# Gate and up products of a decoder's feed-forward blocks: seven block products in place of eight

## The chip, the cores and the metric

One core of a Trainium2 chip runs the whole kernel. The metric is the device time of one execution in microseconds (us). Matrix products run on TensorE (PE for the matmuls, PEld for their weight loads), elementwise work on VectorE (DVE) and ScalarE (ACT), a few DMA starts on GpSimd (POOL); SyncE (SP) starts the other DMAs.

## The reference, cut to what matters

Two layers, each with a feed-forward block, a mixer of four branches, and a second feed-forward block; x is 512 tokens by 1024 features, in float32, and D_FF is 2816.

```python
def _swiglu(x, w_gate, w_up, w_down):
    return (jax.nn.silu(x @ w_gate) * (x @ w_up)) @ w_down
...
for l in range(DEPTH):
    x = x + 0.5 * _swiglu(_rmsnorm(x, ffn1_norm[l]), ffn1_w_gate[l], ffn1_w_up[l], ffn1_w_down[l])
    ...
    x = x + 0.5 * _swiglu(_rmsnorm(x, ffn2_norm[l]), ffn2_w_gate[l], ffn2_w_up[l], ffn2_w_down[l])
```

The change touches `x @ w_gate` and `x @ w_up` in the four feed-forward blocks.

## The kernel before, in words

Activations lie transposed: x is eight tiles of 128 features by 512 tokens. Every float32 operand is split into a high part rounded to float32r and a low rest (`split`, L228: a cast on ACT, a subtraction on DVE), and a product is three matmuls (`mm3`, L223): high by high, high by low, low by high. Each matmul loads 128x128 weights and streams 512 tokens past them.

A feed-forward block (`ffn`, L327) has 22 tiles of 128 hidden features. For one tile, `proj` (L303) makes the gate product and the up product, 8 x 3 matmuls each, into two banks of the pool "mm" (4 banks; another 4 are "bg"). `hidden` (L330) multiplies both by the row factor of the norm (`st.rb`), applies silu, multiplies, and splits the result into two `L` tiles. After 12 tiles, and after the other 10 (`HALVES`, L30), `down` (L315) multiplies the hidden tiles by `w_down` into four banks at a time and adds them to x. The last `down` of a block also prepares the input of the next stage (`norm_split`, L269), and a small generator computes its row factor. In the mixer, `renorm` (L292) rewrites the split input during the third projection.

Weights come as chunks of 128x1024 (512 KB). `nextw` (L215) hands out the next one and keeps two more in work: `load_one` (L181) starts the DMA into one of two `ws` buffers and splits it into one of three `wh` and three `wl`. A buffer comes free when its last reader is through: `wh` and `wl` when the matmuls of that chunk are, `ws` when the subtraction is. At the start of the first block `setup` (L372) builds the attention bias with a DMA to DRAM (`toep`, L389) and back.

The order in which each engine takes its instructions is not that of the program: the library's planner runs through the program with costs of its own, gives each engine the earliest written instruction that is then ready, and that order is fixed in the queues. Waits are on semaphores; an instruction that waits holds all behind it in its queue.

Of the kernel before, what the change touches and what calls it, by code (L numbers as in the profile page):

```python
# [13 lines left out]
F32 = mybir.dt.float32  # L15
# [14 lines left out]
HALVES = ((0, 12), (12, 22))  # L30
# [36 lines left out]
def _trunk(tc, xin, wst, wa, wv, wf, par, relb, cst, out):  # L67
# [8 lines left out]
    def T(shape, dt, tag, bufs=1):  # L76
        uid[0] += 1
        n = int(np.prod(shape[1:])) * (2 if dt == BF16 else 4)
        return (odd if n % 2048 else sb).tile(shape, dt, tag=tag, bufs=bufs, name=f"{tag}_{uid[0]}")
# [18 lines left out]
    def LT(i, dt=F32R):  # L98
        return T([P, S], dt, f"L{i}")
# [60 lines left out]
    sched = []  # L160
    ci = 0
    per_ffn = 2 * NF + 2 * (NF // 2)
    for l in range(2):
        stream = ["w"] * per_ffn
        for z in ZORDER:
            stream += [z] * 4 if z in GROUPS else ["w"]
        stream += ["w"] * (4 * (2 + 8) + 8 + per_ffn)
        kc = {z: 4 * l for z in GROUPS}
        for z in stream:
            if z == "w":  # L170
                sched.append((1024, wst[ci]))
                ci += 1
            else:
                sched.append((2 * GROUPS[z], wg[z][kc[z]]))
                kc[z] += 1
    assert ci == nchunk
    loaded = deque()
    pos = [0]
    AHEAD = 2

    def load_one():  # L181
        n, src = sched[pos[0]]
        pos[0] += 1
        st = T([P, 1024], F32, "ws", 2)[:, 0:n]
        wh = T([P, 1024], F32R, "wh", 3)[:, 0:n]
        wl = T([P, 1024], F32R, "wl", 3)[:, 0:n]
        nc.sync.dma_start(st, src)
        split(wh, wl, st)
        loaded.append((wh, wl))

    def load_first():

        ts_ = []
        for i in range(2):
            pos[0] += 1
            ts_.append((T([P, 1024], F32, "ws", 2), T([P, 1024], F32R, "wh", 3), T([P, 1024], F32R, "wl", 3)))
# [15 lines left out]
        loaded.extend(t[1:] for t in ts_)  # L212
        spawn(norm_end(st))

    def nextw():  # L215
        while len(loaded) <= AHEAD and pos[0] < len(sched):
            load_one()
        return loaded.popleft()
# [49 lines left out]

    def norm_split(st, k):  # L269
        g = pc(st.l, st.off + k)  # L270
        hi = T([P, S], F32R, f"xh{k}")
        lo = T([P, S], F32R, f"xl{k}")
# [19 lines left out]
    def renorm(st):  # L292

        st.x = []
        for k in range(KD):
            y = TP()
            hi = T([P, S], F32R, f"xh{k}")
            lo = T([P, S], F32R, f"xl{k}")
# [28 lines left out]
    def ffn(st, nxt, fin=None, first=False):  # L327
        for hi_, (t0, t1) in enumerate(HALVES):
            hs = []
            def hidden(t, pg, pu, rb):  # L330
                sg, us = TP(), TP()
                V.tensor_mul(sg, pg, rb)  # L332
                A.activation(sg, sg, AF.Silu)
                V.tensor_mul(us, pu, rb)  # L334
                V.tensor_mul(us, us, sg)  # L335
                i = 2 * (t - t0)
                h, hl = LT(i), LT(i + 1)
                split(h, hl, us)
                hs.append((h, hl))

            for t in range(t0, t1):
# [4 lines left out]
                else:  # L346
                    proj(st, wg, pg)
# [3 lines left out]
                hidden(t, pg, pu, st.rb)  # L351
                tick()
            last = hi_ == 1
# [10 lines left out]
            if last and nxt is not None:  # L364
                spawn(norm_end(nxt))

# [27 lines left out]
    def mixer(l, st, nxt):  # L394

# [3 lines left out]
        def conv_tap(c, j):  # L399
            def go():  # L400
                w, src = pc(l, O_DW + c * 31 + j), uu[c][:, j:j + S]
                if j == 0:
                    cacc[c] = T([P, S], F32, f"cacc{c}")
# [6 lines left out]
        def glu(c, pa, pb):  # L410
# [7 lines left out]
            u = T([P, 30 + S], F32, f"u{c}")  # L418
# [86 lines left out]
        def fox_unit(h, i):  # L505
# [16 lines left out]
                if i == 0:  # L522
                    ptile["h"] = T([P, 2048], F32R, "pth").rearrange("p (q j c) -> p q j c", q=4, j=4)
                    ptile["l"] = T([P, 2048], F32R, "ptl").rearrange("p (q j c) -> p q j c", q=4, j=4)
# [31 lines left out]
        def swa_unit(pr, n):  # L556
# [25 lines left out]
                if n == 0:  # L582
                    stile["h"] = T([P, 2048], F32R, "pth").rearrange("p (h s c) -> p h s c", h=2, s=8)
                    stile["l"] = T([P, 2048], F32R, "ptl").rearrange("p (h s c) -> p h s c", h=2, s=8)
# [33 lines left out]
        vh, vl = T([P, NB, 384], F32R, "vh"), T([P, NB, 384], F32R, "vl")  # L618
# [77 lines left out]
        def evacuate(z, ps):  # L696
# [5 lines left out]
            elif z in ("sc0", "sc1"):  # L702
                su = T([P, 2 + S], F32, "su")
# [77 lines left out]
        spawn(norm_end(nxt))  # L781

# [59 lines left out]
def _arrays(i):  # L842
    chunks, groups = [], {z: [] for z in GROUPS}

    def ffn(l, n):
        g, u = _tiles_k8(i[f"ffn{n}_w_gate"][l]), _tiles_k8(i[f"ffn{n}_w_up"][l])
        d = _tiles_k2(i[f"ffn{n}_w_down"][l])
        for t0, t1 in HALVES:
            for t in range(t0, t1):
                chunks.extend([g[t], u[t]])  # L850
# [68 lines left out]
```

## Time and profile before

| | |
|---|---|
| time, median of 3 runs | 2303.49 us (2302.65 to 2303.55) |
| the profiled execution | 2302.64 us, its span 2300.6 us |
| PE, PEld, DVE, ACT busy | 100%, 83%, 51%, 35% of the span |
| granted TensorE clock | 1.000 |
| feed-forward block 1 / mixer of layer 0 | about 12 to 382 us / 382 to 802 us |

A busy share is the time in which the engine has an instruction in work. Matmuls overlap each other, so a matmul's own duration (390 ns for 512 columns) is not what it costs: that is the distance from its start to the start of the next, its pitch, which the timeline shows.

### The profile page before, as it was taken

The numbers are of one execution on the slowest core, as the hardware profiler recorded it, in microseconds if no ns is written. First come the engines' busy times: TensorE is split into PE (matmuls) and PEld (weight loads), VectorE is DVE, ScalarE is ACT, GpSimd is POOL, SyncE is SP. The second block draws the span as 40 slices with busy tenths as digits, with TensorE's granted clock in tenths as the row PEclk, the third lists the DMA queues.
The fourth block names the chain that finished last, engine by engine and source line by source line (L and its number), as shares of the span: only waits on it lengthen the run. The fifth ranks groups of instructions, "written<-read, shape, count | busy, mean of one in ns | idle before, by whom it ended". The sixth has DMA issues, their size and how long they took to land.

```text
span 2300.6 us, 25938 instructions
## 1 busy us (share of the span) xinstructions
PE 2290.1 (100%) x10467; PEld 1898.5 (83%) x10467; DVE 1182.5 (51%) x1790; ACT 801.0 (35%) x1190; POOL 3.8 (0%) x9
## 2 busy tenths in 40 slices
PE   9999999999999999999999999999999999999999
PEld 6788888988888888888888888888888888888887
DVE  5433436676764544344454434466767645442442
ACT  4322224464433333223232223345544334231221
POOL 0000000000000000000000000000000000000000
PEclk9999999999999999999999999999999999999999
DMA  5423332322223333333333332322222333333232
GB/s 145 125 93 100 95 98 78 106 76 78 68 92 93 100 101 92 101 96 96 101 92 97 96 98 94 97 87 91 83 74 65 93 101 98 97 97 101 92 101 92
DMA packets 62120, 217.44 MB, mean 95 GB/s; under 512 B 7408, under 2 KB 7540, under 8 KB 62000
## 3 DMA queue, kind: packets, MB, share of 16 engines
q1 hardware_dynamic: 61056, 214.41, 30.2%
q0 software_dynamic: 944, 1.37, 0.4%
q8 instruction: 82, 1.34, 0.2%
q14 instruction: 38, 0.31, 0.0%
HBM read 212.87 MB, written 2.88 MB: 94 GB/s over the span
## 4 chain that ended last, share of the span: by engine, by line
PE 98%; DMA 2%; ACT 0%; DVE 0%; issue 0%; SPq 0%; ACTq 0%; DVEq 0%
PE mm L224 31%; PE mm L226 31%; PE mm L225 31%; DMA ws<-wst 1%; PE bg L529 0%; PE bg L689 0%; PE bg L513 0%; PE bg L248 0%; PE bg L590 0%; DMA x<-xin 0%; PE bg L545 0%; PE bg L511 0%; PE bg L546 0%; PE bg L544 0%; PE bg L514 0%; PE bg L224 0%
## 5 line engine op out<-in xcount | busy, mean ns | idle before, releaser
L229 ACT CAST wh<-ws 128x1024 fp32r<-128x1024 f32 (+1 forms) x406 | 421.7, 1040 | 1177.5 <-PE mm L225 890.9
L224 PE MATMUL mm<-xh,wh 128*128 128x512 f32 x2080 | 812.8, 392 | 3.4 <-ACT wh L229 3.4
L226 PE MATMUL mm<-xh,wl 128*128 128x512 f32 x2080 | 811.5, 390 | 1.6 <-DVE wl L230 1.6
L225 PE MATMUL mm<-xl,wh 128*128 128x512 f32 x2080 | 810.2, 390 | 0.7 <-DVE xl L135 0.6
L230 DVE TENSOR_TENSOR wl<-ws,wh 128x1024 fp32r<-128x1024 f32 (+1 forms) x406 | 489.6, 1207 | 530.9 <-ACT wh L229 525.5
L226 PEld LDWEIGHTS mm<-xh,wl 128*128 128x128 f32 x2080 | 390.5, 188 | 87.0 <-DVE wl L230 6.0
L224 PEld LDWEIGHTS mm<-xh,wh 128*128 128x128 f32 x2080 | 390.4, 188 | 86.7 <-ACT wh L229 5.4
L225 PEld LDWEIGHTS mm<-xl,wh 128*128 128x128 f32 x2080 | 390.7, 188 | 82.3 <-DVE xl L135 1.5
L226 PE MATMUL mm<-L,wl 128*128 128x512 f32 x960 | 373.6, 389 | 0.0
L224 PE MATMUL mm<-L,wh 128*128 128x512 f32 x960 | 373.5, 389 | 0.0
L225 PE MATMUL mm<-L,wh 128*128 128x512 f32 x960 | 373.5, 389 | 0.0
L226 PEld LDWEIGHTS mm<-L,wl 128*128 128x128 f32 x960 | 180.2, 188 | 37.4
L224 PEld LDWEIGHTS mm<-L,wh 128*128 128x128 f32 x960 | 180.2, 188 | 37.4
L225 PEld LDWEIGHTS mm<-L,wh 128*128 128x128 f32 x960 | 180.2, 188 | 37.3
L334 DVE TENSOR_TENSOR tp<-mm,L 128x512 f32<-128x512 f32 x88 | 60.8, 691 | 268.1 <-PE mm L226 268.1
L332 DVE TENSOR_TENSOR tp<-mm,L 128x512 f32<-128x512 f32 x88 | 60.8, 691 | 182.5 <-PE mm L226 182.4
L135 DVE SCALAR_TENSOR_TENSOR cacc<-u,par,cacc 128x512 f32<-128x512 f32 x120 | 89.0, 742 | 23.3 <-PE mm L226 22.8
L229 ACT CAST L<-tp 128x512 fp32r<-128x512 f32 x96 | 59.9, 624 | 57.1 <-DVE tp L335 56.9
L224 PE MATMUL mm<-wh,xh 128*128 128x384 f32 (+2 forms) x192 | 69.3, 361 | 0.0
L225 PE MATMUL mm<-wl,xh 128*128 128x384 f32 (+2 forms) x192 | 68.1, 355 | 0.0
L226 PE MATMUL mm<-wh,xl 128*128 128x384 f32 (+2 forms) x192 | 68.1, 354 | 0.0
L135 DVE SCALAR_TENSOR_TENSOR x<-mm,x 128x512 f32<-128x512 f32 x80 | 54.5, 687 | 24.8 <-PE mm L226 24.2
(172 smaller groups left out, 1256.6 us busy)
## 6 DMA issues: line engine op xcount, KB each, us to landing
ws<-wst SPq DMA_DIRECT2D x378, 512.0 KB, 3.5
ws<-wf SPq DMA_DIRECT2D x8, 512.0 KB, 3.5
ws<-wv SPq DMA_DIRECT2D x8, 388.0 KB, 3.1
ws<-wa SPq DMA_DIRECT2D x8, 384.0 KB, 3.1
x<-xin SPq DMA_DIRECT2D x8, 256.0 KB, 5.5
out<-x SPq DMA_DIRECT2D x8, 256.0 KB, 2.3
ws<-wst SPq DMA_DIRECT2D x4, 256.0 KB, 5.4
toep<-tp POOLq DMA_DIRECT2D x1, 768.0 KB, 33.8
```

The source lines that it names most:

```text
L135: return V.scalar_tensor_tensor(out=o, in0=i0, scalar=s, in1=i1, op0=a, op1=b)
L224: mm(ps, lhsT=w[0], rhs=xx[0], start=first, stop=False)
L225: mm(ps, lhsT=w[0], rhs=xx[1], start=False, stop=False)
L226: unit[0] = mm(ps, lhsT=w[1], rhs=xx[0], start=False, stop=last)
L229: A.copy(o_hi, src)
L230: V.tensor_sub(o_lo, src, f(o_hi))
L332: V.tensor_mul(sg, pg, rb)
L334: V.tensor_mul(us, pu, rb)
```

## The change

Of the 22 tiles of a block, the first four stay as they were. The other 18 are taken as nine quads: two tiles t and t+1, gate and up together. With the 1024 input features cut into halves, the weights of a quad are four blocks of 512 x 256 (A11, A12 of tile t, A21, A22 of tile t+1; the 256 columns are the gate's 128 and the up's 128), and the input is four blocks of 512 features x 256 tokens (B11 to B22). Instead of the eight block products, seven are made, on sums of the blocks (S1 to S4 of weights, T1 to T4 of inputs), and the results are put together from three accumulators. A block product is 2 x 4 x 3 matmuls of 256 tokens. `halves` makes the input blocks once in a block, while tiles 0 to 3 run, with the row factor multiplied in. Sums of weights are made on DVE before the split; seven splits in a quad take the place of four. The tiles go to `down` in three segments (8, 8, 6) instead of two. The 512 KB weight chunks of a quad are as many as before (four).

The split of the stage's input now lies in eight tiles X0 to X7 of 128x1024, each pair of tiles holding two k (`xpair`); in quads the same tiles take raw weights (X0 to X4) and sums (X5 to X7). Tiles that only the feed-forward blocks or only the mixer use now live in pools that are opened and closed with the stage.

```diff
-HALVES = ((0, 12), (12, 22))
+SEGS = ((0, 8), (8, 16), (16, 22))
+NSTD = 4
+B11, B21, B22, T1, T3, T2, T4 = range(0, 1792, 256)
...
+    RW, RX = ("ws0", "ws1"), tuple(f"X{i}" for i in range(5))
+    HW, LW, HE, LE = ("h0", "h1", "h2"), ("l0", "l1", "l2"), ("h3", "h4"), ("l3",)
+    def item(kind, n, srcs, q=False, raw=RW, a1=None, turn=0):
+        items.append((kind, n, srcs, raw, q, a1 or (4 if q else 2), 3 if q else 2, turn))
...
+        chunk("A11", q=True)
+        for t0, t1 in SEGS:
+            for t in range(max(t0, NSTD), t1, 2):
+                kw = dict(q=True, raw=both, turn=f0)
...
+                    chunk("A12", q=True)
+                chunk("S2", 2, a1=None if q else 2, **kw)
+                item("S3", 1024, [], **kw)
+                item("S1", 1024, [], **kw)
...
+                    chunk("A11", **kw)
+                item("S4", 1024, [], **kw)
+                item("A22", 1024, [], **kw)
...
+    def make_head(i):
...
+        if kind == "S2":
+            blk["A21"], blk["A22"] = r
+            s1, s2 = T([P, 1024], F32, "X5"), T([P, 1024], F32, "X6")
+            V.tensor_add(s1, *r)
+            V.tensor_add(s2, s1, blk["A11"])
+            blk["S1"], blk["S2"], src = s1, s2, s2
+        elif kind == "S3":
+            src = T([P, 1024], F32, "X7")
+            V.tensor_add(src, blk["A11"], blk["A21"])
+        elif kind == "S4":
+            src = blk["S2"]
+            V.tensor_add(src, src, blk["A12"])
...
+        A.copy(hi, src)
...
+    def make_rest(i):
...
+        V.tensor_sub(lo, src, f(hi))
...
+    def nextw():
+        n = turn[0]
+        while True:
+            i, j = p1[0], p2[0]
+            if i < len(items) and i <= n + items[i][5] and i - j < 2:
+                make_head(i)
+                while pr[0] < len(items) and pr[0] <= i + 3 and items[pr[0]][7] and items[pr[0]][7] <= n:
+                    load_raw(pr[0])
+            elif j < i and j <= n + items[j][6]:
+                make_rest(j)
+            else:
+                break
...
+    def xpair(st, k):
+        if k % 2 == 0:
+            st.pair = [T([P, 2 * S], F32R, f"X{k + i}") for i in range(2)]
+        return [t[:, S * (k % 2):S * (k % 2) + S] for t in st.pair]
...
+        def halves(k):
...
+            for i in range(2):
+                stt(y[:, S * i:S * i + S], x[k + 4 * i], pc(st.l, st.off + k + 4 * i), st.rb, ALU.mult, ALU.mult)
+            b = [y[:, 256 * i:256 * i + 256] for i in range(4)]
+            split(th[k][:, B11:B11 + 256], tl[k][:, B11:B11 + 256], b[0])
+            V.tensor_sub(ta[:, 0:256], b[0], b[1])
+            V.tensor_sub(ta[:, 256:S], b[1], b[3])
+            A.copy(th[k][:, B21:B21 + S], y[:, S:2 * S])
+            A.copy(th[k][:, T1:T1 + S], ta)
+            stt(tb[:, 0:256], ta[:, 0:256], -1.0, b[3], ALU.mult, ALU.subtract)
+            V.tensor_add(tb[:, 256:S], b[2], tb[:, 0:256])
+            A.copy(th[k][:, T2:T2 + S], tb)
+            for o, src in ((B21, y[:, S:2 * S]), (T1, ta), (T2, tb)):
+                V.tensor_sub(tl[k][:, o:o + S], src, f(th[k][:, o:o + S]))
+        def product(ps, w, o, first=False):
+            for s in range(2):
+                for k in range(4):
+                    c = slice(256 * k + P * s, 256 * k + P * s + P)
+                    d, t0, t1 = ps[:, 256 * s:256 * s + 256], th[k][:, o:o + 256], tl[k][:, o:o + 256]
...
+        def begin():
+            w, a, c11 = nextw(), PSB(), SP()
+            product(a, w, B11, True)
+            A.copy(c11, a)
+            return a, c11
...
+        def quad(t):
+            a, c11 = nxtq[0] or begin()
+            w, b = nextw(), PSM()
+            product(b, w, B21, True)
+            V.tensor_add(c11, c11, b)
+            w = nextw()
+            product(a, w, T2)
+            cc = T([P, 2 * S], F32, "cc", 2, pool="ffn").rearrange("p (s h c) -> p s h c", s=2, h=2)
+            A.copy(cc[:, :, 0, :], gu(a))
+            w, c = nextw(), PSM()
+            product(c, w, T3, True)
+            w = nextw()
+            product(a, w, T1)
+            A.copy(cc[:, :, 1, :], gu(a))
+            V.tensor_sub(cc[:, :, 1, :], gu(c), cc[:, :, 1, :])
+            nxtq[0] = begin() if t + 2 < NF else None
+            w = nextw()
+            product(a, w, B22)
+            sg = TP()
+            A.activation(sg[:, 0:256], c11[:, 0:256], AF.Silu)
+            A.activation(sg[:, 256:S], a[:, 0:256], AF.Silu)
+            V.tensor_mul(sg[:, 0:256], sg[:, 0:256], c11[:, 256:S])
+            V.tensor_mul(sg[:, 256:S], sg[:, 256:S], a[:, 256:S])
+            put(sg)
+            w = nextw()
+            product(c, w, T4)
+            V.tensor_sub(cc[:, :, 0, :], gu(c), cc[:, :, 0, :])
+            sg = TP()
+            A.activation(sg, cc[:, 0].rearrange("p h c -> p (h c)"), AF.Silu)
+            V.tensor_mul(sg, sg, cc[:, 1].rearrange("p h c -> p (h c)"))
+            put(sg)
```

## Rows read from the trace of the kernel before

**Rows 1.** The page: busy time of each engine, and the chain of work that ended last, by engine.
```profile
PE 2290.1 (100%) x10467; PEld 1898.5 (83%) x10467; DVE 1182.5 (51%) x1790; ACT 801.0 (35%) x1190; POOL 3.8 (0%) x9
...
PE 98%; DMA 2%; ACT 0%; DVE 0%; issue 0%; SPq 0%; ACTq 0%; DVEq 0%
```
**Rows 2.** The waits, PE alone (us in total, times, longest), and one row of the waits of the weight loads.
```profile
PE mm L224 <- ACT wh L229: 3.4, 4, 1.9
PE mm L226 <- DVE wl L230: 1.6, 3, 0.5
...
PEld mm L225 <- DVE xl L230: 0.7, 2, 0.3
```
**Rows 3.** The timeline of PE in a gate and up stretch (start in us, duration in us): the first and the last of 13 matmuls of 512 columns.
```profile
300.13 0.39 PE L224 MATMUL mm<-xh,wh 128*128 128x512 f32 x1
...
302.85 0.39 PE L224 MATMUL mm<-xh,wh 128*128 128x512 f32 x1
```
**Rows 4.** The same in the mixer: the first and the last of 24 matmuls of 256 columns in a row, and after them the weight loads of the second and the last of these (PEld).
```profile
489.89 0.28 PE L609 MATMUL bg<-pth,vh 128*128 128x256 f32 x1
...
492.65 0.28 PE L611 MATMUL bg<-pth,vl 128*128 128x256 f32 x1
...
489.90 0.19 PEld L610 LDWEIGHTS bg<-ptl,vh 128*128 128x128 f32 x1
...
492.53 0.19 PEld L611 LDWEIGHTS bg<-pth,vl 128*128 128x128 f32 x1
```
**Rows 5.** Busy time of each engine around that place: PE, PEld, DVE, ACT, POOL in us (x instructions), the granted clock, the DMA share, GB/s.
```profile
483.20:493.40 10.20, 10.20 (x65) 8.64 (x63) 9.50 (x31) 6.37 (x15) 0.00 (x0) 1.00 0.15 52
```
**Rows 6.** The groups of DVE by shape (busy us, mean ns of one, idle before).
```profile
L230 DVE TENSOR_TENSOR wl<-ws,wh 128x1024 fp32r<-128x1024 f32 x386 | 471.6, 1223 | 529.1 <-ACT wh L229 523.9 <-PE mm L226 5.1
...
L678 DVE TENSOR_TENSOR L<-L,sm 128x256 f32<-128x256 f32 x16 | 5.5, 419 | 0.0
```
**Rows 7.** The timeline of DVE in a gate and up stretch, four instructions in a row; then a piece of the mixer's `renorm`.
```profile
299.65 0.69 DVE L334 TENSOR_TENSOR tp<-mm,L 128x512 f32<-128x512 f32 x1 [3.31 <-PE mm L226]
300.44 0.69 DVE L335 TENSOR_TENSOR tp<-tp,tp 128x512 f32<-128x512 f32 x1
301.05 1.22 DVE L230 TENSOR_TENSOR wl<-ws,wh 128x1024 fp32r<-128x1024 f32 x1
302.19 0.68 DVE L230 TENSOR_TENSOR L<-tp,L 128x512 fp32r<-128x512 f32 x1
...
392.25 0.75 DVE L135 SCALAR_TENSOR_TENSOR tp<-x,par,L 128x512 f32<-128x512 f32 x1
392.91 0.69 DVE L230 TENSOR_TENSOR xl<-tp,xh 128x512 fp32r<-128x512 f32 x1
```
**Rows 8.** The timeline of ACT: two instructions of the start, two of a gate and up stretch, one that follows on DVE's work; and the copies and activations from PSUM by shape (busy us, mean ns).
```profile
8.60 0.62 ACT L284 ACTIVATE tp<-x 128x512 f32<-128x512 f32 x1
9.12 0.71 ACT L273 ACTIVATE xh<-x,par 128x512 fp32r<-128x512 f32 x1
...
294.02 1.05 ACT L229 CAST wh<-ws 128x1024 fp32r<-128x1024 f32 x1 [3.11 <-PE mm L225]
294.98 0.62 ACT L333 ACTIVATE tp<-tp 128x512 f32<-128x512 f32 x1
...
301.17 0.63 ACT L229 CAST L<-tp 128x512 fp32r<-128x512 f32 x1 [0.65 <-DVE tp L335]
...
L256 ACT COPY L<-bg 128x512 f32<-128x512 f32 x6 | 3.5, 585 | 36.4 <-PE bg L255 36.4
...
L673 ACT COPY L<-mm 128x256 f32<-128x256 f32 x16 | 5.2, 382 | 0.8 <-PE mm L226 0.8
```
**Rows 9.** DMA issues by line (KB each, median us to landing).
```profile
ws<-wst SPq DMA_DIRECT2D x378, 512.0 KB, 3.5
...
toep<-tp POOLq DMA_DIRECT2D x1, 768.0 KB, 33.8
```
**Rows 10.** The timeline of POOL, DVE and ACT in the first block: the start of the `toep` transfer, what DVE did just before it, and the casts of the weight chunks 8 to 11, counted from 0 (in brackets the wait before).
```profile
33.75 1.15 POOL L389 DMA_DIRECT2D toep<-tp  x1 [16.59 <-DVE tp L386]
...
32.90 0.55 DVE L386 TENSOR_TENSOR tp<-bg,tp 4x384 f32<-4x384 f32 x1
...
55.71 1.04 ACT L229 CAST wh<-ws 128x1024 fp32r<-128x1024 f32 x1 [15.77 <-DMA ws<-wst]
...
62.62 1.05 ACT L229 CAST wh<-ws 128x1024 fp32r<-128x1024 f32 x1 [5.35 <-DMA ws<-wst]
...
68.92 1.05 ACT L229 CAST wh<-ws 128x1024 fp32r<-128x1024 f32 x1 [4.72 <-DMA ws<-wst]
...
70.39 1.04 ACT L229 CAST wh<-ws 128x1024 fp32r<-128x1024 f32 x1
```
**Rows 11.** The timeline of PE there: the last matmul of chunk 7, the first and third of chunk 8, the last of chunk 8 and the first of chunk 9.
```profile
54.48 0.39 PE L226 MATMUL mm<-xh,wl 128*128 128x512 f32 x1
56.81 0.50 PE L224 MATMUL mm<-xh,wh 128*128 128x512 f32 x1 [1.94 <-ACT wh L229]
...
58.07 0.50 PE L226 MATMUL mm<-xh,wl 128*128 128x512 f32 x1 [0.53 <-DVE wl L230]
...
62.97 0.39 PE L226 MATMUL mm<-xh,wl 128*128 128x512 f32 x1
63.72 0.50 PE L224 MATMUL mm<-xh,wh 128*128 128x512 f32 x1 [0.37 <-ACT wh L229]
```

More of the change, by code (lines that the diff above doesn't have):

```diff
@@ L74, in _trunk, with T, open_stage @@
     uid = [0]
-    def T(shape, dt, tag, bufs=1):
+    stage = {}
+    def T(shape, dt, tag, bufs=1, pool=None):
         uid[0] += 1
         n = int(np.prod(shape[1:])) * (2 if dt == BF16 else 4)
-        return (odd if n % 2048 else sb).tile(shape, dt, tag=tag, bufs=bufs, name=f"{tag}_{uid[0]}")
+        pool = stage[pool] if pool else odd if n % 2048 else sb
+        return pool.tile(shape, dt, tag=tag, bufs=bufs, name=f"{tag}_{uid[0]}")
+    def open_stage(*names):
+        cx = ExitStack()
+        for n in names:
+            uid[0] += 1
+            stage[n] = cx.enter_context(tc.tile_pool(name=f"{n}{uid[0]}", bufs=1))
+        return cx
     def PSM():
@@ L163, in _trunk @@
     for l in range(2):
-        stream = ["w"] * per_ffn
+        ffn_items()
+        kc = {z: 4 * l for z in GROUPS}
         for z in ZORDER:
[L166 to L172, printed above, removed]
-            else:
-                sched.append((2 * GROUPS[z], wg[z][kc[z]]))
-                kc[z] += 1
+            if z in GROUPS:
+                for _ in range(4):
+                    item("w", 2 * GROUPS[z], [wg[z][kc[z]]])
+                    kc[z] += 1
+            else:
+                chunk()
@@ L176, in _trunk @@
+        for _ in range(4 * (2 + 8) + 8):
+            chunk()
+        ffn_items()
     assert ci == nchunk
[L177 to L189, printed above, removed]
+    used, seq = {}, [0]
@@ new lines, in place, with wtile, load_raw @@
+    def place(names):
+        n = min(names, key=lambda m: used.get(m, 0))
+        seq[0] += 1
+        used[n] = seq[0]
+        return n
+    raws, heads, ready = {}, {}, {}
+    pr, p1, p2, turn = [0], [0], [0], [0]
+    blk = {}
+    def wtile(names, dt):
+        n = place(names)
+        if n in HE + LE:
+            return T([P, 1024], dt, n, pool="ffn")
+        return T([P, 1024], dt, *((n,) if n in RX else (n[:-1], 2 if n in RW else 3)))
+    def load_raw(i):
+        kind, n, srcs, raw = items[i][:4]
+        raws[i] = []
+        for src in srcs:
+            t = wtile(raw, F32)[:, 0:n]
+            nc.sync.dma_start(t, src)
+            raws[i].append(t)
+        pr[0] = i + 1
@@ L211, in load_first @@
                 norm_split(st, k)
[L212 removed]
+        for i in range(2):
+            ready[i] = ts_[i][1:]
         spawn(norm_end(st))
[L215 to L218, printed above, removed]
     def kt(w, c=P):
@@ L327, in ffn @@
     def ffn(st, nxt, fin=None, first=False):
[L328 to L341, printed above, removed]
+        cx = open_stage("ffn", "tf")
@@ new lines, in gu, with put, hidden @@
+        def gu(t):
+            return t.rearrange("p (s c) -> p s c", s=2)
+        def begin():
[3 more added lines that the diff above has]
+            return a, c11
+        nxtq = [None]
+        hs = []
+        def put(us):
+            i = 2 * len(hs)
+            h, hl = (T([P, S], F32R, f"hs{j}", pool="ffn") for j in (i, i + 1))
+            split(h, hl, us)
+            hs.append((h, hl))
+        def hidden(pg, pu, rb):
+            sg, us = TP(), TP()
+            V.tensor_mul(sg, pg, rb)
+            A.activation(sg, sg, AF.Silu)
+            V.tensor_mul(us, pu, rb)
+            V.tensor_mul(us, us, sg)
+            put(us)
@@ L342, in ffn @@
+        for t0, t1 in SEGS:
+            hs.clear()
+            for t in range(t0, min(NSTD, t1)):
                 wg, wu = kt(nextw()), kt(nextw())
@@ L346, in ffn @@
                 else:
+                    halves(t)
                     proj(st, wg, pg)
@@ L350, in ffn @@
                     spawn(setup())
-                hidden(t, pg, pu, st.rb)
+                if t == 0:
+                    halves(0)
+                hidden(pg, pu, st.rb)
                 tick()
-            last = hi_ == 1
+            for t in range(max(NSTD, t0), t1, 2):
+                quad(t)
+                tick()
+            last = t1 == NF
             def after(d, ps):
```

97 lines of the change are left out of this document (76 added, 21 removed).

## The prediction

> **What bounds the kernel now.** I read the page first, then the waits of PE, then the timeline of PE for pitches, then DVE and ACT by shape and in time, and last the first 75 us. The reader is to see on the page that PE has work throughout and makes 98% of the chain that ended last [rows 1]: nothing shortens this kernel but fewer or faster matmuls. The waits say that PE alone lost some 5 us to the others' lateness [rows 2]. DVE and ACT have half and two thirds of their time free, on the mean over all stages; the gate and up stretches are what counts here.
>
> The price of a matmul is its pitch. Twelve steps of 512 columns take 302.85 - 300.13 = 2.72 us, 226.7 ns each [rows 3]; 23 steps of 256 columns take 492.65 - 489.89 = 2.76 us, 120.0 ns each, with a fresh weight load for every one [rows 4]. The difference, 106.7 ns for 256 columns, leaves 13.3 ns per matmul that do not shrink with the columns. The 190 ns in a weight load's record are no occupancy: those of rows 4 start 120 ns apart as well (22 steps in 2.63 us).
>
> **What is removed and added on PE.** Two tiles cost 2 x 48 matmuls of 512 columns before, 96 x 226.7 ns = 21.76 us. A quad has 7 x 24 = 168 of 256 columns, 168 x 120.0 ns = 20.16 us, 2.88 us per product. An eighth of the columns goes (2.56 us per quad) and 72 more matmuls at 13.3 ns give 0.96 us back: 1.60 us gained, and for 4 blocks of 9 quads 57.6 us. `down` and the four plain tiles keep their matmuls. This gain is small beside what the other engines may add, so their part decides.
>
> **DVE and ACT in a quad.** Back to back, a 1024 element subtraction occupies DVE for 1.14 us (301.05 to 302.19), a 512 element one for 0.61; an instruction that needs the one before it starts 0.79 after it, not 0.61 [rows 7]. A 256 element one lasts 419 ns [rows 6], 0.34 as a pitch by the same 0.08 us of overlap. A quad gives DVE seven splits and four sums of weights (11 x 1.14 = 12.5), the sum into c11 and two differences (3 x 0.61 = 1.8), two products of 256 and one of 512 (1.3), and two splits of hidden tiles (1.2), with 0.2 for the sum that follows on a sum: 17.0 us of the 20.16 that PE needs, 84%. ACT has seven casts at 0.96, three copies from PSUM at about 0.5, silu on 512 and twice on 256 (1.3) and two casts at 0.52 [rows 8]: 10.5 us, 52%. Neither is the bound by its sum. What can stop PE is order. An accumulator `a` is copied out by ACT and used again by PE one product later, three times in a quad: there ACT has 2.88 us, for a copy of 0.58 and at most one cast of 1.05 ahead of it. Weights have more room: a rest is begun when the product before last frees its buffer and is needed three products (8.6 us) later. The planner does not keep to the program's order: DVE at 301.05 takes the next chunk's subtraction ahead of the hidden tile's, which was written earlier but waits for a cast [rows 7]. So a sum of weights is taken as soon as its inputs are there and does not stand in front of the copies. For what remains of bad order I bound the stall of PE per quad by 0 below (no row excludes it) and by 1.7 us above (the first rival), and take 0.2, near the lower end, because DVE has 3 us spare per quad: 7 us in all.
>
> **Start of the quads.** S2 needs two raw chunks in X tiles that hold the split input of the plain tiles until the last projection has read them. The first pair is free after 6 of its 24 matmuls, 4.1 us before its end; two loads then land 3.5 us later or somewhat more [rows 9], near that end. Two dependent sums (2.5 us), a cast (1.0) and the subtraction (1.2) are 4.7 us, beside 2 to 3 us of DVE for the last plain tile; PE comes to that product 5.76 us after the projection. `halves` adds to DVE in each plain tile 2 x 0.66 [rows 7], 5 x 0.34 and 3 x 0.61, 4.9 us, beside some 4.9 that are there (two rests at 1.14, four of 512): 9.8 of PE's 10.9, and all of it waits for the row factor, so DVE ends late by one or two us. I take 1 us for each of blocks 2 to 4 (0 to 4): 3 us.
>
> **The first block.** There the `toep` transfer runs from 33.75 for 33.8 us [rows 9, 10], and weight loads beside it take 10 to 20 us: chunk 8 was cast at 55.71 after 15.8 us of waiting, chunk 9 at 62.62, chunk 10 at 68.92, chunk 11 by 70.39 [rows 10]. Before, PE lost 2.1, 0.7 and 0.5 us to this [rows 11], because tile 4 needed only chunks 8 and 9 for its 10.9 us. A quad needs all four within 5.76 us. A11 could start at 56.8 and end at 60.4; A12 from 63.7 to 67.3; S2 has its chunks at 70.4, then 2.5 of sums and 1.1 of cast: 74.0, with 0.9 more for the rest. Idle: 2.8 + 4.0 + 7.6 = 14.4, less the 3.3 of before: 11 us. The extra loads in flight could share the time better (8), or `toep` itself could start later, since the instruction that releases it (32.90, DVE [rows 10]) now stands behind two `halves`, up to 7 us (18). I take 13.
>
> **The rest.** `renorm` rewrites a tile that holds two k, so it starts one k (3 x 226.7 = 0.7 us) later, in a place where PE already waited 0.7 us for it [rows 2]: 2 x 0.7 = 1.4 us. The third segment adds eight 0.69 us additions to x on DVE, where `down` leaves it nearly idle (5.44 us of PE for 1.14 of split); if that cover failed each would be late, not PE. Tiles in pools opened per stage are first written after PE has had 5 us of the new stage, and all readers of the old are then through: 0, and were that wrong, some us at each of the five later openings. DMA bytes are the same.
>
> **The sum.** 2302.6 (the profiled execution, 0.85 under the median) - 57.6 + 7 + 3 + 13 + 1.4 = 2269.4, so 2270, 1.4% faster. Its own range, with the ends above and 0 to 0.5 us per quad: 2254 to 2294.
>
> **Rivals.** First, **the loop through the accumulator**, which ends slower. Were DVE to take its work nearly as written, the copy that frees `a` before the S1 product would stand behind ACT's cast of S4, that behind DVE's sum for S4, and that behind the end of the previous quad. From the start of the S1 product: 2.88 to its end and 0.7 for the copy; DVE then has a difference, three sums, three rests, two products, a hidden split with its cast, about 10.1 us without a gap, to the last difference of the quad; from there 0.8, silu 0.6, product 0.8, cast 0.7, splits 0.6 and 1.14, c11 0.6, the S4 sum 1.2, cast 1.0, copy 0.6, 8.1 us. Together 21.8 us per quad, 1.7 over PE's, and no gain at all: with the other terms 2302.6 + 36 x 0.1 + 17 = 2323. It decides from 1.1 us of stall per quad ((57.6 - 17.4)/36), at which the time is as before. For it: DVE at 84%, and semaphores between three engines. Against it: the order in rows 7, and that the loop's members have 3 us of slack. 12%.
>
> Second, **a dense stream is slower than rows 4**. The closest packing that the trace shows for long is 24 matmuls; over 65 matmuls it has 157 ns each [rows 5], for other reasons perhaps. Each ns of pitch is 168 x 36 = 6.0 us; at 124 ns the forecast becomes 2294, and from 125.4 ns it is slower than before; at 157 it would be 2493. Against it: in rows 4 nothing drifts between the first and the last step. 7%. [...]
>
> Third, **all is hidden**: the loads beside `toep` share their time, and order costs nothing: 2302.6 - 57.6 + 1.4 = 2246. For it: PE lost only 5 us before, with the same engines. Against it: the four chunks that the first quad needs at once. 16%.
>
> **Chances.** The forecast 65%, the loop 12%, the dense stream 7%, all hidden 16%. Two kernels within 0.2%, 4.6 us, can't be told apart here. Faster: 16 + 64 + 5 from the low ends of the other two: 85%. Within 0.2%: 5%. Slower: 10%. The range that leaves out some 2 in 10 goes from all hidden to the upper end of the forecast and a milder form of the loop: 2246 to 2304.
>
> **What would show it.** PE's timeline in a quad: 256 column matmuls 120 ns apart, 24 in 2.88 us (the dense stream shows at once, in every product). PE's waits: rows on ACT's and DVE's tiles; if the S1, B22 or T2 products wait for copies into `cc` or `c11` the loop is there. DVE near 84% in a quad stretch. In the first 85 us, PE idle 10 to 20 us, ended by a DMA or by the sums behind one. In blocks 2 to 4 a gap of about 1 us before the first S2 product. The prediction is wrong if stalls inside quads exceed 20 us in total, or if the pitch differs from 120 by over 2 ns.

## The result, and the profile after

The changed kernel takes 2274.31 us (median of 4 runs, 2272.3 to 2276.64), beside 2303.08 us before: ratio 0.9875, 95% interval 0.9858 to 0.9892. It is 1.25% faster. The profiled execution took 2276.64 us, its span 2274.9 us. Of the page, the busy times, the granted clock in 40 slices and the chain, to be held against [rows 1]:

```profile
PE 2234.0 (98%) x13059; PEld 1973.6 (87%) x13059; DVE 1542.3 (68%) x2234; ACT 1004.0 (44%) x1506; POOL 3.8 (0%) x9
...
PEclk9699999999999999999999999999999999999999
...
PE 95%; DMA 2%; DVE 1%; ACT 1%; issue 0%; SPq 0%; ACTq 0%; DVEq 0%
```

PE is still the bound, but one slice, the second (57 to 114 us), stands out: the clock there has a 6. The waits of PE name who held it, where [rows 2] had 5 us in all (`h` and `l` are the high and low parts of a weight chunk, `th` and `tl` those of the input blocks that `halves` makes; line numbers are those of each run's own kernel):

```profile
PE bg L483 <- ACT h L292: 22.2, 7, 11.7
PE bg L483 <- ACT th L352: 8.6, 1, 8.6
PE mm L483 <- ACT h L292: 3.3, 4, 1.5
...
PE bg L486 <- DVE l L299: 0.6, 2, 0.5
```

Some 35 us, in 14 waits, all in the block products. To place them I took from the timeline of PE the length of each stage, from its first matmul to that of the next:

| stage | before | after | difference |
|---|---|---|---|
| feed-forward block 1 | 369.6 | 380.1 | +10.5 |
| blocks 2, 3, 4 | 360.5 each | 348.2, 346.5, 349.7 | -12.3, -14.0, -10.8 |
| the two mixers | 419.9 each | 419.9, 419.8 | 0 |

Before, by the same reading, block 1 runs from 6.0 to 375.6 us and the first mixer to 795.5; the times given ahead of the prediction are some 6 us too late.

Inside a segment of quads away from its start nothing is lost. The timeline of PE in the second segment of block 2, two matmuls 24 apart:

```profile
962.19 0.28 PE L483 MATMUL mm<-th,h 128*128 128x256 f32 x1
...
965.02 0.28 PE L483 MATMUL mm<-th,h 128*128 128x256 f32 x1
```

That is 117.9 ns per matmul, and the whole segment of four quads keeps it, as the busy time by stretches shows (PE, PEld, DVE, ACT, POOL in us, with the number of instructions; the granted clock; DMA share; GB/s). The second stretch is the start of block 1's first quads:

```profile
943.10:1022.10 79.00, 79.00 (x672) 78.99 (x671) 62.50 (x69) 43.71 (x58) 0.00 (x0) 1.00 0.32 101
54.80:100.00 45.20, 19.13 (x95) 17.45 (x95) 24.69 (x34) 14.62 (x21) 0.78 (x1) 0.62 0.42 114
```

From its first matmul (943.11) to that of the next stage (1022.26) the segment takes 79.15 us: 117.8 ns for each of the 672, a quad in 79.15 / 4 = 19.79 us. Against the 21.76 us of two plain tiles that is 1.97 us gained per quad, 17.7 per block. Blocks 2 to 4 fall short of it by 5.4, 3.7 and 6.9 us, and block 1, which is 10.5 us longer and not 17.7 shorter, by 28.2. With these the sum is 2302.64 (the execution of before) - 36 x 1.97 + 16.0 + 28.2 + 0.9 (the first projection starts 0.86 us later) = 2276.8, measured 2276.64. As the losses were read from the stage lengths, this shows only that nothing was lost outside the feed-forward blocks.

**Block 1.** On the timeline of PE, the first four waits of the quads, the first matmul of the second product (79.04), and two matmuls nine steps apart (80.96 and 82.88):

```profile
66.94 0.58 PE L483 MATMUL bg<-th,h 128*128 128x256 f32 x1 [11.70 <-ACT h L292]
68.20 0.58 PE L486 MATMUL bg<-th,l 128*128 128x256 f32 x1 [0.47 <-DVE l L299]
78.66 0.58 PE L483 MATMUL bg<-th,h 128*128 128x256 f32 x1 [8.60 <-ACT th L352]
79.04 0.41 PE L483 MATMUL mm<-th,h 128*128 128x256 f32 x1
80.96 0.41 PE L483 MATMUL bg<-th,h 128*128 128x256 f32 x1
82.88 0.41 PE L483 MATMUL bg<-th,h 128*128 128x256 f32 x1
91.19 0.39 PE L483 MATMUL bg<-th,h 128*128 128x256 f32 x1 [4.77 <-ACT h L292]
```

The wait of 8.60 us lies inside the first product: its fourth k needs the `th` of `halves(3)`. The matmuls at 80.96 and 82.88 are 1.92 / 9 = 0.213 us apart; between them the granted clock is 0.50, where the segment above has 1.00. These four waits and one of 0.53 us behind them are 26.1 us, 22.8 more than the 3.3 of before; 54 matmuls of this stretch stand 0.213 us apart, 54 x 0.0955 = 5.2 us. The two make 28.0 of the 28.2.

ACT in that time (the casts of weights are L292, the others make `th`):

```profile
46.95 0.62 ACT L469 CAST th<-cc 128x512 fp32r<-128x512 f32 x1 [0.26 <-DVE cc L159]
65.84 1.04 ACT L292 CAST h<-ws 128x1024 fp32r<-128x1024 f32 x1 [18.27 <-DMA ws<-wst]
66.79 0.61 ACT L470 CAST th<-sp 128x512 fp32r<-128x512 f32 x1
72.88 1.04 ACT L292 CAST h<-ws 128x1024 fp32r<-128x1024 f32 x1 [5.48 <-DMA ws<-wst]
73.83 0.61 ACT L473 CAST th<-sp 128x512 fp32r<-128x512 f32 x1
```

Read the third row with the second. The input of the `th` cast, a difference on DVE, was done at 47.9; the cast ran at 66.79, because a weight cast stood in front of it that waited 18.27 us for its load. The planner has put the two weight casts into the middle of `halves(2)`. DVE stands until 66.92 at the low part of that chunk, then until 74.48 for the next `th`, and `halves(3)` stands behind it. The load itself was issued at 43.92, when the subtraction at 42.64 had freed its buffer; the load of the same chunk went out at 35.21 before, behind a subtraction at 33.97. The timeline of the DMA queue on SP, before and then after:

```profile
35.21 0.33 SPq L187 DMA_DIRECT2D ws<-wst  x1
...
43.92 0.33 SPq L265 DMA_DIRECT2D ws<-wst  x1
```

It landed 21.9 us after its issue (20.4 before), beside `toep`, which started at 42.4 in place of 33.75 and took 36.2 us, 2.4 more than in [rows 9]. The DMA issues from 20 to 100 us (median us to landing):

```profile
ws<-wst SPq DMA_DIRECT2D x8, 512.0 KB, 3.6
X<-wst SPq DMA_DIRECT2D x6, 512.0 KB, 24.0
toep<-tp POOLq DMA_DIRECT2D x1, 768.0 KB, 36.2
```

**Blocks 2 to 4.** The timeline of DVE, and then of PE, at the start of block 2's quads:

```profile
853.60 0.68 DVE L510 TENSOR_TENSOR tp<-mm,L 128x512 f32<-128x512 f32 x1
855.27 1.23 DVE L278 TENSOR_TENSOR X<-X,X 128x1024 f32<-128x1024 f32 x1 [0.99 <-DMA X<-wst]
856.41 0.68 DVE L511 TENSOR_TENSOR tp<-tp,tp 128x512 f32<-128x512 f32 x1
857.01 1.22 DVE L279 TENSOR_TENSOR X<-X,ws 128x1024 f32<-128x1024 f32 x1
...
859.65 0.39 PE L483 MATMUL bg<-th,h 128*128 128x256 f32 x1 [1.44 <-ACT h L292]
861.64 0.39 PE L483 MATMUL mm<-th,h 128*128 128x256 f32 x1 [1.49 <-ACT h L292]
...
863.17 0.42 PE L483 MATMUL bg<-th,h 128*128 128x256 f32 x1
864.67 0.41 PE L485 MATMUL bg<-tl,h 128*128 128x256 f32 x1
```

The first sum for S2 waits for the raw tiles in X, which were issued from 847.72 on and are there 3.4 us after the last projection ended (851.83). PE could have begun the product at 857.5 (851.83 and two products of 2.83); it began at 859.65. And behind the gap the clock is lower: matmuls 214 ns apart (863.17 to 864.67, seven steps), with a granted clock of 0.50 between them. The timeline has some 40 such matmuls in blocks 2 and 4 and none in a row in block 3, about 4 us of the 16.0.

### The profile page after: what moved, and what is told of

It reads as the page before. It is cut to its first block, busy times and chain, and to the rows that moved or that the text cites. A ratio compares the mean times of both kernels' runs of the same rounds, so it can differ in the third digit from the quotient of the medians.

```text
span 2274.9 us, 31903 instructions
## 1 busy us (share of the span) xinstructions
PE 2234.0 (98%) x13059; PEld 1973.6 (87%) x13059; DVE 1542.3 (68%) x2234; ACT 1004.0 (44%) x1506; POOL 3.8 (0%) x9
## 4 chain that ended last, share of the span: by engine, by line
PE 95%; DMA 2%; DVE 1%; ACT 1%; issue 0%; SPq 0%; ACTq 0%; DVEq 0%
PE mm L347 20%; PE mm L349 20%; PE mm L348 20%; PE bg L483 6%; PE bg L486 6%; PE bg L485 6%; PE mm L483 4%; PE mm L486 4%; PE mm L485 4%; DMA ws<-wst 1%; DMA X<-wst 1%; PE bg L746 0%; PE bg L906 0%; PE bg L730 0%; PE bg L371 0%
## 5 line engine op out<-in xcount | busy, mean ns | idle before, releaser
L299 DVE TENSOR_TENSOR l<-ws,h 128x1024 fp32r<-128x1024 f32 (+2 forms) x246 | 295.9, 1204 | 345.8 <-ACT h L292 276.6
L292 ACT CAST h<-X 128x1024 fp32r<-128x1024 f32 x264 | 277.3, 1053 | 442.3 <-PE mm L348 193.1
L299 DVE TENSOR_TENSOR l<-X,h 128x1024 fp32r<-128x1024 f32 x264 | 320.7, 1221 | 186.0 <-PE mm L349 74.3
L292 ACT CAST h<-ws 128x1024 fp32r<-128x1024 f32 (+2 forms) x246 | 255.0, 1038 | 429.8 <-PE mm L348 256.3
L347 PE MATMUL mm<-X,h 128*128 128x512 f32 x928 | 364.2, 395 | 0.6 <-ACT h L352 0.5
L349 PE MATMUL mm<-X,l 128*128 128x512 f32 x928 | 363.0, 391 | 0.0
L348 PE MATMUL mm<-X,h 128*128 128x512 f32 x928 | 361.8, 391 | 0.7 <-DVE X L159 0.6
L483 PE MATMUL bg<-th,h 128*128 128x256 f32 x1152 | 327.1, 284 | 30.9 <-ACT h L292 22.2
L486 PE MATMUL bg<-th,l 128*128 128x256 f32 x1152 | 325.4, 283 | 0.6 <-DVE l L299 0.6
L485 PE MATMUL bg<-tl,h 128*128 128x256 f32 x1152 | 325.2, 282 | 0.0
L347 PE MATMUL mm<-hs,h 128*128 128x512 f32 x704 | 274.1, 389 | 0.0
L348 PE MATMUL mm<-hs,h 128*128 128x512 f32 x704 | 273.9, 389 | 0.0
L347 PEld LDWEIGHTS mm<-X,h 128*128 128x128 f32 x928 | 174.2, 188 | 38.3 <-ACT h L352 1.6
L348 PEld LDWEIGHTS mm<-X,h 128*128 128x128 f32 x928 | 174.4, 188 | 37.6 <-DVE X L159 1.5
```

What stands on the lines that cost most here:

```text
L292: A.copy(hi, src)
L299: V.tensor_sub(lo, src, f(hi))
L347: mm(ps, lhsT=w[0], rhs=xx[0], start=first, stop=False)
L348: mm(ps, lhsT=w[0], rhs=xx[1], start=False, stop=False)
L349: unit[0] = mm(ps, lhsT=w[1], rhs=xx[0], start=False, stop=last)
L483: mm(d, lhsT=w[0][:, c], rhs=t0, start=first and s == 0 and k == 0, stop=False, skip_group_check=True)
```

## Experiments

Two theories at the outset. **D**: block 1 loses because weight loads land late beside the `toep` transfer. **V**: quads lose by the work that they add to DVE and ACT (`halves`, the sums of S1 to S4). "Less" below is against the 2274.31 us of the changed kernel. Every kernel was timed beside the kernel before on the same chip (2302.25 us for e1 to e4, 2302.69 for e5 to e8, 2302.92 for e9 and e10, 2302.86 for e11).

**e1, block 1 with eight plain tiles.**

```diff
+STD = (8, 4, 4, 4)
...
-            for t in range(t0, min(NSTD, t1)):
+            for t in range(t0, min(nstd, t1)):
```

> The first block keeps 8 plain tiles in place of 4 (its first segment has no quads), so that its quads begin after the toep transfer (78.6 us in the changed kernel). Theory D (the first block loses some 29 us because weight chunks land 10 to 20 us late beside toep): the loss in that block falls to the 5 us or so that plain tiles lost before, less two quads' gain (4 us): 2276.6 - 34 + 5 + 4, about 2252 us. Theory V (the first block loses because halves and its casts load DVE and ACT): the four halves stand where they stood, so the stall only moves to the plain tiles or stays: 2270 to 2280.

Measured: 2257.8 us (2256.32 to 2261.33), ratio 0.9808 [0.9793, 0.9823]. It has two quads fewer than the changed kernel and is 16.5 us faster. But the loss did not go: the eight plain tiles took 109.74 us where 8 x 10.88 = 87.0 would do. The longest wait of PE (us in total, times, longest):

```profile
PE mm L350 <- DVE tp L512: 13.3, 1, 13.3
```

and the timeline of ACT in that stretch:

```profile
65.31 1.04 ACT L295 CAST h<-ws 128x1024 fp32r<-128x1024 f32 x1 [17.97 <-DMA ws<-wst]
```

A plain tile stalls 13.3 us on DVE, behind the same cast. So neither theory has it whole: the stall is tied to the transfer, but not to quads. The quads of block 1, which here come behind a down projection, lost nothing: 696 matmuls in 81.98 us, 117.8 ns each.

**e2, without the transfer** (the bias is left out, set to zero).

```diff
...
-        nc.gpsimd.dma_start(dst, br[0:4, 0:384]...)
...
-        nc.gpsimd.dma_start(bias, src)
+        V.memset(bias, 0.0)
```

> The two transfers of the attention bias (to DRAM and back) are left out and the bias is set to zero; all else is the changed kernel. Theory D: the first block comes down to what block 3 takes, 346.5 us from 380.1: 2243 us, and its four halves take DVE no longer than in the other blocks. Theory V: the gaps before the first products of quad 1 stay, above 2265.

Measured: 2247.95 us (two executions, 2247.87 and 2248.03), ratio 0.9763 [0.9744, 0.9783]: 26.4 us less. D holds for most of the 28.2 us. What is left lies at the start of the quads: the first segments take 51.82 us in block 1 and 44.74, 45.72 and 48.94 in the others, where 360 x 117.8 ns = 42.4 would do. The three in blocks 2 to 4, which the edit does not touch, lose 12.2 us here and 15.8 in the changed kernel; over the runs that leave these blocks alone (e1, e2, e3, e5, e9, e11) it is 11.6 to 15.8. Differences of up to 4 us there are no effect of an edit.

**e3, the transfer moved into the first mixer.**

```diff
-                if first and t == 0:
-                    spawn(setup())
...
+        if l == 0:
+            spawn(setup())
```

> The bias is built at the start of the first mixer in place of the first block. Theory D: the first block as in the run without toep (2243), plus what the transfer costs in the mixer, whose chunks are asked for every 5.4 us as in the plain tiles of the kernel before, where it cost 4 to 5 us: 2243 to 2249. Theory V: above 2265.

Measured: 2270.43 us (2269.54 to 2271.4), ratio 0.9861 [0.9846, 0.9876]: D's 2243 to 2249 is missed, and the number is V's for another reason. Block 1 did fall to 353.6 us, but the mixer rose by 21.5 (441.4 for 419.9). There the timeline of ACT shows the pattern again:

```profile
397.39 0.83 ACT L292 CAST h<-ws 128x768 fp32r<-128x768 f32 x1 [18.40 <-DMA ws<-wa]
```

and that of PE what it costs:

```profile
398.80 1.22 PE L347 MATMUL mm<-X,h 128*128 128x512 f32 x2 [17.81 <-ACT X L352]
```

PE waits for a cast of `renorm` whose input was ready; the weight cast in front of it waits for a load. The price goes where the transfer goes.

**e4, the last plain tile's gate and up projections in turn,** so that X tiles come free earlier.

```diff
+                    if t == NSTD - 1:
+                        for k in range(KD):
+                            for w, ps in ((wg, pg), (wu, pu)):
+                                mm3(ps, (w[0][:, k, :], w[1][:, k, :]), st.x[k], ...)
...
```

> The last plain tile of each block takes gate and up k by k in turn, so that the X tiles come free 8.2, 5.4, 2.7 and 0 us before its end in place of 4.1, 2.7, 1.4 and 0. Theory D for blocks 2 to 4 (the raw chunks A21 and A22 land late, at 855.3 where the product is due at 857.7, and the half clock follows from the gap): the stalls of 5.3, 3.6 and 6.8 us go to 0 to 1.5 each: 12 us less, about 2263. Theory V (DVE is behind by the halves until 854.3, so S2 is late anyway): under 4 us less. The first block is not helped by it in either.

Measured: 2266.9 us (2265.16 to 2267.97), ratio 0.9843 [0.9826, 0.9859], 7.4 us less. The raw loads went out 8.2 us before the end of the last plain tile (842.30 of 850.50) in place of 4.1 (847.72 of 851.83), and the first segments of blocks 2 to 4 took 44.86, 44.57 and 46.09 us. That is a loss of 8.3 us, below all the runs that leave these blocks alone (11.6 to 15.8), but half of the changed kernel's stayed, with gaps of 0.7 and 1.2 us and DVE busy without a break: both the loads and DVE's queue are in it.

**e5, the same transfer from 128 partitions.** The four rows of the bias are made 32 times over by the matmul, and each partition writes a 32nd.

```diff
-        mm(ps[0:4, 0:384], lhsT=rt, rhs=oh[0:32, 0:384], start=True, stop=True)
+        mm(ps[:, 0:384], lhsT=r4, rhs=oh[0:32, 0:384], start=True, stop=True)
...
-        dst = bass.AP(..., ap=[[P * 385, 4], [385, P], [1, 384]])
+        dst = bass.AP(..., ap=[[4 * 385, P], [385, 4], [1, 384]])
```

> The bias transfer `toep` writes the same bytes, but from 128 partitions in place of 4 (the 4 rows are made 32 times over by the matmul that makes them). Theory D (the first block's loss comes from the weight loads that land late beside `toep`, since they share the DMA engines that the 4 partitions use): as the kernel without the bias, 2248 us (2246 to 2252), `toep` well under 20 us, block 1 near 354 us. Rival B (the bytes as such, 786 KB written and 512 KB read back, are what delays the loads, however they are spread): 2262 to 2275 us, with casts of ACT that still wait 10 us or more on a load in the first block.

Measured: 2252.78 us (2251.06 to 2253.47), ratio 0.9782 [0.9768, 0.9797]: 21.5 us less, 0.8 over D's range and far from B's. The timeline of POOL:

```profile
42.22 0.74 POOL L607 DMA_DIRECT2D toep<-tp  x1 [24.94 <-DVE tp L604]
49.46 0.79 POOL L609 DMA_DIRECT2D bias<-toep  x1 [6.50 <-DMA toep<-tp]
```

and of ACT, the cast that waited 18 us:

```profile
49.69 1.05 ACT L292 CAST h<-ws 128x1024 fp32r<-128x1024 f32 x1 [2.31 <-DMA ws<-wst]
```

The transfer starts where it did and takes 7.0 us. Its bytes, which are the same, were not the price; what the edit changed is the number of source partitions, and with it the order in which the rows are written. By what path the slow transfer held the loads beside it no run shows.

**e6, a down projection ahead of the first quad.**

```diff
-SEGS = ((0, 8), (8, 16), (16, 22))
+SEGS = ((0, 4), (4, 10), (10, 16), (16, 22))
...
```

> Segments of 4, 6, 6 and 6 tiles in place of 8, 8 and 6: the four plain tiles get their own down projection, and the first product of the first quad comes behind it, in all four blocks; the same matmuls in another order. Theory V (in blocks 2 to 4 the first quad loses because its raw tiles X and its sums on DVE can only be made once the last plain projection is done): with 22 us of down projection between the two, the segments of quads in blocks 2 to 4 have no gap and stay at full clock, 5.3 + 3.6 + 6.8 = 15.7 us less, about 2258 us; in block 1 it changes little or helps by up to 10 us (2248 to 2260). Rival S (a first quad stalls wherever it begins, because its S2, S3, S1 sums and casts follow one upon the other on DVE and ACT): 2270 to 2278 us, with the same gaps of 1.2 to 1.5 us before the third and fourth product.

Measured: 2258.2 us (2257.37 to 2260.06), ratio 0.9808 [0.9793, 0.9823]. The waits at the start of the quads are gone in blocks 2 to 4, which take 344.17 us each (342.8 without loss; each has one new wait of 1.06 us, ahead of its last down projection's first matmul). In block 4's stretch, by busy times, PE is busy throughout, at the upper clock:

```profile
1970.00:1985.00 15.00, 15.00 (x111) 14.23 (x110) 12.95 (x15) 5.49 (x7) 0.00 (x0) 1.00 0.28 101
```

S falls. The time is as V had it, but by a somewhat other sum: 4.0 + 2.3 + 5.5 = 11.8 us in blocks 2 to 4, and 6.9 in block 1 (373.2).

**e7, e5 and e6 together.**

> The two edits together: `toep` from 128 partitions, and a down projection ahead of the first quad. Theory D with V: the losses are separate places, so the sum is near ideal: 2248 less 21.5 (what the kernel without the bias still lost in its first segments of quads: 9.4, 2.3, 3.3 and 6.5) = 2227 us (2224 to 2234), with TensorE idle under 12 us in all. If either B or S is right, 2240 us or more.

Measured: 2236.9 us (2235.6 to 2237.79), ratio 0.9714 [0.9699, 0.9728]: 37.4 us less than the changed kernel, a gain more than twice as large over the kernel before. The two edits add up (21.5 + 16.1 = 37.6). It is 2.9 us over the expected range: block 1 takes 352.4 us, still 8.2 more than the others. Not all of that comes with the change: in the kernel before the first block was 9.1 us longer than the others too (369.6 beside 360.5, 3.3 of it in the waits of [rows 11]).

**e8, dead matmuls in the gaps** of blocks 2 to 4: `dead(12)` makes twelve matmuls whose result nobody reads.

```diff
...
+            if t == NSTD and not first:
+                dead(12)
             product(a, w, T2)
...
+            if t == NSTD and not first:
+                dead(12)
             product(c, w, T3, True)
```

> In blocks 2 to 4 twelve matmuls whose result nobody reads stand before the third and again before the fourth product of the first quad, 12 x 117.7 ns = 1.41 us each, where TensorE now waits 1.2 to 1.5 us: 8.5 us of work in all. Theory C (about half of the 15.7 us that these blocks lose is the granted clock at its lower level behind the gaps, the rest the gaps themselves, 2.93, 2.58 and 3.17 us): the gaps are filled, the clock stays at its upper level, and the time falls by up to 7 us, to 2267 to 2270 us. Rival N (the products behind the gaps are slow for another reason, such as a wait that the trace shows as a longer matmul): no gain or the added work in full, 2274 to 2283 us.

Measured: 2271.97 us (2270.99 to 2272.86), ratio 0.9868 [0.9851, 0.9884], 2.3 us less, between the two. The stretch of block 4 by busy times, first in the changed kernel:

```profile
1970.00:1985.00 15.00, 11.83 (x71) 11.05 (x71) 12.45 (x13) 7.58 (x10) 0.00 (x0) 0.77 0.43 155
```

and here:

```profile
1970.00:1985.00 15.00, 13.64 (x113) 13.44 (x114) 15.00 (x16) 9.01 (x12) 0.00 (x0) 1.00 0.43 141
```

C's mechanism is there: 1.00 in place of 0.77. But the time does not decide between C and N. With 8.5 us of added work and 4.5 of loss that stayed (46.14, 46.93 and 47.15 us for 384 matmuls, 45.24 without loss) the three segments spend 13.0 us over their useful work, within the 11.6 to 15.8 of the runs that leave them alone.

**e9, `toep` one tile earlier,** and **e10, the same in e7.**

```diff
         yield
-        yield
         ps = PSB()
```

> The changed kernel with `setup` resumed one tile earlier: the add that releases `toep` stands behind one `halves` on DVE in place of two, so the transfer from 4 partitions starts 10 us or more sooner (42.4 us so far), and ends near 65 us in place of 78.6. Theory E (the price in the first block is how far the window of `toep` reaches into the quads, which ask for a weight chunk every 2.83 us where plain tiles ask for one every 5.44 us): the first block loses about 20 us in place of 34, the time falls to 2256 to 2264 us. Rival A (what counts is that a cast of ACT waits for a load and holds the casts behind it, whichever tile it meets): the wait only moves into the plain tiles, 2268 to 2276 us.

Measured: 2273.54 us (2270.96 to 2275.57), ratio 0.9873 [0.9859, 0.9886]: as A had it, no gain from 9 us of lead (the transfer started at 33.39). The timelines of this kernel show best of all what a queue does. ACT:

```profile
56.44 1.04 ACT L292 CAST h<-ws 128x1024 fp32r<-128x1024 f32 x1 [18.03 <-DMA ws<-wst]
57.39 0.61 ACT L473 CAST th<-sp 128x512 fp32r<-128x512 f32 x1
```

DVE:

```profile
39.56 0.67 DVE L508 TENSOR_TENSOR tp<-mm,L 128x512 f32<-128x512 f32 x1
58.03 0.69 DVE L475 TENSOR_TENSOR tl<-sp,th 128x512 fp32r<-128x512 f32 x1 [17.80 <-ACT th L473]
58.64 0.68 DVE L510 TENSOR_TENSOR tp<-mm,L 128x512 f32<-128x512 f32 x1
59.24 1.22 DVE L299 TENSOR_TENSOR l<-ws,h 128x1024 fp32r<-128x1024 f32 x1
```

and PE:

```profile
60.52 0.80 PE L349 MATMUL mm<-X,l 128*128 128x512 f32 x1 [16.29 <-DVE l L299]
```

PE waits 16.29 us, in a plain tile, for the low part of a chunk whose cast was done at 33.8. The low part ran at 59.24 because DVE stood at 58.03, at a subtraction that waited for a `th` cast, which stood behind the cast of another chunk, whose load was late. No row of PE names that load.

> The kernel with both edits (`toep` from 128 partitions, a down projection ahead of the first quad), with `setup` resumed one tile earlier as well. Its first block still lost about 8 us against the others, with waits on casts between 58 and 70 us. Theory E: the transfer (6.5 us from 128 partitions) then lies in the second plain tile, where loads are asked for at half the rate: 2228 to 2234 us. Rival K (that rest belongs to the start of the block, where `halves` and the hidden tiles fill DVE and ACT, and not to the transfer): no change from 2236.9, 2235 to 2239 us.

Measured: 2236.24 us (2235.48 to 2236.59), ratio 0.9711 [0.9698, 0.9725], as K had it: with this short a transfer, starting one tile earlier changes nothing. What the rest of 8 us in block 1 is was not settled.

**e11, the order alone,** with the transfer from 4 partitions as it was.

```diff
+                early = first and t == 3
+                if early:
+                    halves(t)
                 wg, wu = kt(nextw()), kt(nextw())
...
-        A.copy(hi, src)
+        c = A.copy(hi, src)
+        if paced[0] is not None:
+            tc.add_manual_dep(c.ins, paced[0].ins.name, after_unit, reason="paced")
```

> The changed kernel with the transfer as it was (4 partitions) and two orders moved in the first block: `halves(3)` is issued ahead of the last plain tile's weights, and the casts of the first two weight chunks of the quads are made to stand behind its last `th` cast on ACT, where two of them stood in the middle of `halves(2)`. Theory A (the casts that wait 18 us for a load hold `th` casts, and these hold the low parts and sums on DVE, whose data had long been there): the wait of TensorE for a `th` cast (8.6 us) goes, the first sum for the third product runs before 80 us in place of 87, and the time falls by 6 to 12 us, to 2262 to 2268 us. The first wait, about 12 us for the first chunk itself, stays. Rival L (the late landing of the loads alone sets the four products): the wait moves to the next chunk, 2271 to 2277 us.

Measured: 2267.29 us (2266.47 to 2268.65), ratio 0.9845 [0.9831, 0.9858], 7.0 us less, as A had it. The timeline of ACT:

```profile
55.08 0.62 ACT L476 CAST th<-sp 128x512 fp32r<-128x512 f32 x1 [0.66 <-DVE sp L475]
64.54 1.04 ACT L293 CAST h<-ws 128x1024 fp32r<-128x1024 f32 x1 [8.85 <-DMA ws<-wst]
```

and of DVE:

```profile
78.63 1.23 DVE L279 TENSOR_TENSOR X<-X,X 128x1024 f32<-128x1024 f32 x1 [4.20 <-DMA X<-wst]
```

The last `th` cast is done before the weight cast begins to matter, no wait for `th` is left, and the first sum for S2 runs at 78.63, where it ran at 87.11. Part of the gain moved to the next load (6.2 us, the wait for the second chunk). So the order is the smaller share, 7.0 us; the larger is the late landing, which e5 removes (21.5 us with the order left as it was).

## Why the prediction was right, and where it was not

The forecast was 2270 us and the range 2246 to 2304; 2274.3 lies in it, and "faster" came out: the mechanism, fewer columns on a PE that stays the bound, is the one that was forecast. That the number is so near is luck: two errors of opposite sign meet. Inside the quads the time came out 22 us better than the terms (13.3 by the pitch, 7 by the order, 1.4 by `renorm`), at their starts 29 us worse (13.0, 15.2 and the 0.9 of the later start).

- **The price of a matmul** (57.6 us). Right in kind, mis-sized. The 23 steps of [rows 4] gave 120.0; a stream of 672 gives 117.8. By the prediction's own working that is 226.7 - 117.8 = 108.9 ns for the columns and 8.9 that do not shrink with them, not 13.3, and the quads gained 36 x 1.97 = 70.9 us. By the prediction's own sign (a pitch off by more than 2 ns) this step failed, to the good side.
- **Order inside quads** (7 us). Measured 0: the 79.15 us of four quads have no gap. DVE took 62.50 / 4 = 15.6 us per quad where 17.0 was summed (79% for 84%), ACT 10.9 for 10.5. The sums were good; the 0.2 us per quad, put in with no row for it, was not needed.
- **Start of the quads in blocks 2 to 4** (3 us). Measured 16.0, over the stated 12 (the least of the other runs, 11.6, is nearly four times the 3). The step that failed: "two loads then land 3.5 us later or somewhat more [rows 9], near that end". Five loads go out within 3.9 us from 847.72 and the pair is summed at 855.27, 3.4 us past the end of the projection; the hidden tile's work on DVE comes between the sums. The clock behind the gap (0.50) was not thought of at all, about 4 us here. e6 shows that the place is right: with a down projection between, the gaps are gone.
- **The first block** (13 us). Measured 28.2. The step that failed is the list of arrivals: "A11 could start at 56.8", "A12 from 63.7", S2 at 74. They started at 66.9, 79.0 and 91.2. The list took the loads' times from before, and counted each chunk by its own load. But A11's load went out 8.7 us later, since its buffer comes free by a subtraction that now stands behind `halves`; that `toep` itself would start later was in the text, as the upper end. So the first two chunks were cast at 65.84 and 72.88, some 10 us behind the list. The rest is order: the first product's fourth k, with the second product behind it, and the sum for the third stood behind casts and sums held in ACT's and DVE's queues (e9, e11). That DVE has spare time did not help: it stood idle from 48.9 to 66.9 with work in its queue. And some 5 us are the lower clock in this stretch (54 matmuls 0.213 us apart), which the prediction did not have.
- **`renorm`** (1.4 us). Measured 0, by the mixers' lengths.
- **The loop through the accumulator** (12%) and **the dense stream** (7%) fall by the rows of the second segment. No run shows the 124 ns at which the second rival has 2294 us: the 672 matmuls in a row there have 117.8 ns each. (The loop's own sum, 21.8 - 20.16, is 1.6 us over PE's time and not 1.7.) **All hidden** (16%) falls by the first block; e7 is the kernel in which it nearly comes true: 2236.9 us, and below its 2246 because of the pitch.

## What to carry to other kernels

When a change makes an engine ask for its data in a burst (here four chunks within 5.7 us, where the plain tiles take one every 5.44), look first at the one place where the data come late already, and follow the instructions that stand behind the waiting one in each engine's queue, not only the data of the product in question: ACT, idle for 56% of the span, held the other casts for 18 us behind one that waited. A large transfer out of few partitions is worth trying to spread (here 36.2 us from 4, 7.0 from 128, and 21.5 us of time, e5) before anything is moved around it; moving it (e3, e9) only moved the stall. And give a new stage a start whose inputs can be made under the tail of the old one: one down projection moved ahead of the first quad was worth 16.1 us (e6).

## What was not expected of the hardware

- Matmuls of 256 columns, each with weights of its own, hold 117.8 ns over 672 in a row, with a weight load for each beside them (78.99 us busy of 79).
- The same 768 KB took 36.2 us from 4 partitions and 7.0 us from 128, and a 512 KB load issued beside the first landed after 21.9 us, beside the second after 5.9; the eight loads into `ws` from 20 to 100 us of the changed kernel took 3.6 (median), the six into X 24.0.
- The clock fell behind a few short gaps, and not always: block 4's stretch (15 us), with gaps of 1.21, 1.33 and 0.63 us, had a granted clock of 0.77, block 2's (19 us, gaps of 1.44 and 1.49) 0.91, while block 3's (12 us), with 0.49, 1.29 and 0.64, kept 1.00. At the lower level, a granted clock of 0.50, the matmuls were 214 ns apart. The stretches of blocks 2 and 3:

```profile
853.00:872.00 19.00, 16.02 (x119) 15.40 (x118) 16.97 (x18) 9.76 (x13) 0.00 (x0) 0.91 0.47 163
1204.00:1216.00 12.00, 9.43 (x73) 8.61 (x72) 11.98 (x12) 7.92 (x10) 0.00 (x0) 1.00 0.43 154
```
